# Cutting the opening transfers 1, 1, 1, 2, 3 in place of 1, 1, 1, 1, 2, 2 in an RMS-norm and matrix-product kernel

## Chip, cores, metric

The kernel runs on one core of one Trainium2 chip. The metric is the device time of one execution in microseconds (us). The span of a profile is shorter than this time by about 2 us.

## The reference

```python
# x: 16 x 1024 x 512, weight: 512 x 768, all float32
def reference(x, gamma, weight, eps):
    rms = np.sqrt(np.mean(x ** 2, axis=-1, keepdims=True) + eps)
    x_norm = x / rms * gamma
    return np.matmul(x_norm, weight).astype(np.float32)
```

The 16,384 rows are worked in 128 tiles of 128 rows. A tile of x has 256 KB, a tile of the output 384 KB.

## The kernel before

A tile is loaded by SyncE (SP), cast to bfloat16 on GpSimd (POOL), transposed on TensorE (PE) two bfloat16 at a time as one float32 word, and copied back from PSUM by VectorE (DVE). It is then multiplied by the scaled weights on TensorE. ScalarE (ACT) squares and sums the rows and takes the root; VectorE takes the reciprocal. The product is scaled by it on ScalarE (even tiles) or VectorE (odd tiles), and stored by SyncE. All loads and stores of x and the output go through the one queue of SyncE.

The lists below cut the tiles into transfers. The first 16 tiles are packed so that a transfer of n tiles gives each partition n neighbouring rows.

```python
    opening = [1, 1, 1, 1, 2, 2]
    last = NT // OG - 1                                   # NT = 128, XG = 16, OG = 8
    x_first, x_size = stretches(XG, {0: opening + [4, 4], 1: [4, 4, 8], 2: [8, 8]})   # others: 16
    o_first, o_size = stretches(OG, {0: opening, 1: [4, 4], last - 1: [4, 4],
                                     last: [2, 2, 1, 1, 1, 1]})                       # others: 8

    def rows(ap, i, n):
        if i < XG:
            return ap[i * P:(i + n) * P, :].rearrange("(p t) d -> p t d", t=n)
        return ap.rearrange("(g p t) d -> g p t d", p=P, t=XG)[i // XG, :, i % XG:i % XG + n, :]
    # ... cut ...
    def load(i):
        if i // XG not in x_tiles:
            x_tiles[i // XG] = xin.tile([P, XG, D], F32, name="xt")
        nc.sync.dma_start(out=held(x_tiles, XG, i, x_size[i]), in_=rows(x, i, x_size[i]))
    # ... cut ...
    def store(i):
        first, n = o_first[i], o_size[i]
        if i == first + n - 1:
            nc.sync.dma_start(out=rows(out, first, n), in_=held(o_tiles, OG, first, n))
```

The opening, and the head of the loop over pairs of tiles (pair j is tiles 2j and 2j+1):

```python
        load_weights(0)
        load_until(3)
        load_weights(1)
        load_until(2 * XG)
        # ... tiles 0 to 3, each alone; cut ...
        cast(6, nc.gpsimd, 2)
        cast(8, nc.gpsimd, 2)
        norms(4, 2)
        for j in range(2, NP):
            load_until(2 * j + AHEAD)                     # AHEAD = 20
            if j + 3 < NP:
                cast(2 * j + 6, nc.gpsimd, 2)
            if j < 4:
                norms(2 * j + 2, 2)                       # squares, root, reciprocal
            # ... cut ...
            for i, engine in ((2 * j, nc.scalar), (2 * j + 1, nc.vector)):
                a = accumulator()
                matmuls(i, a, range(K), feed)             # feed: transposes a later pair, then its copy
                finish_tile(i, a, engine)                 # scales, and stores when a stretch is full
```

Of the kernel before, what the change touches and what calls it, by code (L numbers as in the profile page):

```python
# [18 lines left out]
def kernel(  # L19
# [32 lines left out]
                i += n  # L52
        return first, size

    opening = [1, 1, 1, 1, 2, 2]
    last = NT // OG - 1
    x_first, x_size = stretches(XG, {0: opening + [4, 4], 1: [4, 4, 8], 2: [8, 8]})
    o_first, o_size = stretches(OG, {0: opening, 1: [4, 4], last - 1: [4, 4], last: [2, 2, 1, 1, 1, 1]})
# [290 lines left out]
```

## Time and profile before

| | before |
|---|---|
| time, median of 3 runs | 211.08 us (210.78 to 211.16) |
| span of the profiled run | 209.0 us |
| TensorE busy | 201.6 us, 96% of the span |
| queue of SyncE | 85.46 MB, 97.0% of 16 DMA engines' span |
| first matmul of tile 6 | 18.16 us, after 0.27 us of idle time |
| last issue of a store | 203.9 us |

A line of a group or a timeline gives start, length, engine, line of the kernel, operation, output <- input, and how many; the bracket is the idle time before it and what ended it. In the rows by slice a digit is the busy share in tenths. The lines that the argument began from stand in the prediction.

### The profile page before, as it was taken

What the parts mean: (1) busy time and instruction counts of PE and PEld (TensorE: products, weight loads), DVE (VectorE), ACT (ScalarE), POOL (GpSimd) and SP (SyncE); (2) the same over time, 40 slices, a digit from 0 to 9 for tenths busy, and PEclk for the clock granted to TensorE, in tenths of its full rate; (3) what the DMA queues carried; (4) which work ended last, traced back from release to release, by engine and by line L of the source; (5) the groups of instructions that cost most, each with busy time, mean ns of one, the idle gap of its engine ahead of it and who ended that gap; (6) DMA issues with size and microseconds to landing.
All of it is one profiled execution on the core that took longest, in us unless ns stands there. A gap on an engine that the chain in (4) does not pass through costs nothing.

```text
span 209.0 us, 3534 instructions
## 1 busy us (share of the span) xinstructions
PE 201.6 (96%) x1298; PEld 137.9 (66%) x1298; DVE 109.0 (52%) x173; ACT 149.6 (72%) x359; POOL 67.0 (32%) x73
## 2 busy tenths in 40 slices
PE   7999999999999999999999999999999999999980
PEld 2466777666766776667766776667667766677640
DVE  0465654654565465456545644654564465456550
ACT  2689987787778778777877777787777778777640
POOL 1357532306331073213623062310633045230000
PEclk9999999999999999999999999999999999999999
DMA  6999999999999999999999999999999999899994
GB/s 231 392 430 422 408 395 436 424 414 439 431 458 411 412 442 425 447 411 437 428 448 419 423 423 442 433 433 417 428 442 447 405 441 414 381 386 386 383 374 182
DMA packets 7077, 85.69 MB, mean 410 GB/s; under 512 B 786, under 2 KB 916, under 8 KB 3476
## 3 DMA queue, kind: packets, MB, share of 16 engines
q1 hardware_dynamic: 7056, 85.46, 97.0%
q8 instruction: 10, 0.16, 0.3%
q14 instruction: 7, 0.06, 0.1%
q10 hardware_dynamic: 4, 0.00, 0.0%
HBM read 35.13 MB, written 50.33 MB: 409 GB/s over the span
## 4 chain that ended last, share of the span: by engine, by line
PE 91%; ACT 3%; DMA 2%; POOL 1%; DVE 1%; issue 0%; SPq 0%
PE ops L168 77%; PE tp L133 13%; DMA xt<-in_x_dram 2%; ACT jk L98 1%; ACT ot L150 1%; POOL xb L94 1%; ACT rms L102 0%; DVE xT L140 0%; PE ops L227 0%; DVE ot L152 0%; SPq L206 0%; DVE rstd L104 0%
## 5 line engine op out<-in xcount | busy, mean ns | idle before, releaser
L168 PE MATMUL ops<-w_bf,xT 128*128 128x256 bf16 (+1 forms) x1024 | 194.2, 326 | 0.3 <-DVE xT L140 0.3
L168 PEld LDWEIGHTS <-xT 128*128 128x128 bf16 x1024 | 100.0, 98 | 56.4 <-DVE xT L140 1.4
L94 POOL CAST xb<-xt 128x1024 bf16<-128x1024 f32 (+1 forms) x67 | 66.3, 1002 | 118.9 <-PE tp L133 72.9
L150 ACT ACTIVATE ot<-ops,rstd 128x768 f32<-128x768 f32 (+1 forms) x65 | 58.1, 894 | 47.2 <-PE ops L168 47.2
L140 DVE COPY xT<-tp 128x1024 bf16<-128x1024 bf16 (+1 forms) x67 | 44.7, 667 | 83.3 <-PE tp L133 83.0
L98 ACT ACTIVATE jk<-xt 128x512 bf16<-128x512 f32 x128 | 78.7, 619 | 0.7 <-DMA xt<-in_x_dram 0.7
L133 PE MATMUL tp<-ident_f,xb 128*128 128x128 f32 x256 | 68.9, 273 | 0.1
L152 DVE TENSOR_SCALAR ot<-ops,rstd 128x768 f32<-128x768 f32 (+1 forms) x65 | 64.5, 993 | 2.9 <-PE ops L168 2.9
L133 PEld LDWEIGHTS tp<-ident_f,xb 128*128 128x128 f32 x256 | 35.9, 141 | 3.8 <-POOL xb L94 0.7
L98 ACT ACTIVATION_READ_ACCUMULATOR jk<-xt 128x1 f32 x128 | 24.4, 191 | 0.0
L102 ACT ACTIVATE rms<-ssq,eps_sb 128x4 f32<-128x4 f32 (+3 forms) x35 | 10.4, 297 | 1.1
L104 DVE RECIPROCAL rstd<-rms 128x4 f32<-128x4 f32 (+3 forms) x35 | 5.9, 167 | 3.3 <-ACT rms L102 3.3
L227 PE MATMUL ops<-warm 128*128 128x512 bf16 x16 | 6.4, 561 | 1.2 <-DVE eps_sb L220 1.2
L227 PEld LDWEIGHTS <-warm 128*128 128x128 bf16 x16 | 1.9, 131 | 3.9 <-issue 2.5
L150 ACT ACTIVATE w_bf<-w_f,g_sb 128x768 bf16<-128x768 f32 x2 | 1.9, 936 | 3.6 <-DMA w_f<-in_weight_dram 3.6
L201 ACT ACT_TABLE_LOAD x1 | 1.3, 1283 | 1.3 <-PEq L330 1.3
L152 DVE TENSOR_SCALAR w_bf<-w_f,g_sb 128x512 bf16<-128x512 f32 (+2 forms) x3 | 1.4, 485 | 1.1 <-DMA w_f<-in_weight_dram 1.0
L241 DVE COPY g_sb<-tp 128x4 f32<-128x4 f32 x1 | 0.2, 162 | 3.1 <-PE tp L239 3.1
L239 PEld LDWEIGHTS tp<-ident_f,g_row 2*128 2x128 f32 x2 | 0.3, 200 | 0.8 <-issue 0.8
L218 DVE MEMSET warm<- 128x256 uint32 x1 | 0.3, 272 | 0.9 <-PEq L330 0.9
L239 PE MATMUL tp<-ident_f,g_row 2*128 2x2 f32 x2 | 0.4, 264 | 0.0
masks.py:199 POOL TENSOR_SCALAR_AFFINE_SELECT ident_f<-ident_f 128x128 f32<-128x128 f32 x1 | 0.3, 292 | 0.1
(6 smaller groups left out, 0.7 us busy)
## 6 DMA issues: line engine op xcount, KB each, us to landing
out_dram<-ot SPq DMA_DIRECT2D x12, 3072.0 KB, 16.3
xt<-in_x_dram SPq DMA_DIRECT2D x5, 4096.0 KB, 23.0
xt<-in_x_dram SPq DMA_DIRECT2D x3, 2048.0 KB, 19.4
out_dram<-ot SPq DMA_DIRECT2D x4, 1536.0 KB, 11.6
xt<-in_x_dram SPq DMA_DIRECT2D x4, 1024.0 KB, 13.2
out_dram<-ot SPq DMA_DIRECT2D x4, 768.0 KB, 10.4
out_dram<-ot SPq DMA_DIRECT2D x7, 384.0 KB, 11.2
w_f<-in_weight_dram SPq DMA_DIRECT2D x2, 768.0 KB, 5.9
```

Of the source, the lines that this page charges most:

```text
L94: engine.tensor_copy(out=xb_tiles[i // 2][:, i % 2:i % 2 + n, :], in_=held(x_tiles, XG, i, n))
L98: nc.scalar.activation(out=jk, in_=held(x_tiles, XG, i)[:, 0, :], func=AF.Square, accum_out=ssq)
L102: nc.scalar.activation(out=rms[:, :n], in_=ssq[:, :n], func=AF.Sqrt, scale=1.0 / D, bias=eps_sb)
L104: nc.vector.reciprocal(out=rstd[:, :n], in_=rms[:, :n])
L133: nc.tensor.transpose(out=tp_tiles[j][:, t, h, :], in_=words[:, lo:lo + P], identity=ident_f)
L140: nc.vector.tensor_copy(out=dst[:, t:t + n, :], in_=src[:, t:t + n, :])
L150: nc.scalar.mul(out=dst, in_=src, mul=r)
L152: nc.vector.tensor_single_scalar(out=dst, in_=src, scalar=r, op=mybir.AluOpType.mult)
L168: nc.tensor.matmul(out=acc[:, lo:hi], lhsT=xT_tiles[i // 2][:, i % 2, k // 2, :, k % 2], rhs=w_bf[:, k, lo:hi], start=(k == 0), stop=(k == ...
L201: nc.scalar.preload_act_table(AF.Sqrt)
L227: nc.tensor.matmul(out=spare[:, :WIDE], lhsT=warm[:, :P], rhs=warm, start=True, stop=True)
L239: nc.tensor.transpose(out=gp[:, c, :], in_=g_row[:, :, c], identity=ident_f[:2, :2])
```

## The change

The intent is to save transfers, and so their fixed costs, in the opening: tiles 3 to 7 are moved in a pair and a triple.

```diff
-    opening = [1, 1, 1, 1, 2, 2]
+    opening = [1, 1, 1, 2, 3]
```

The one list cuts loads and stores alike. Three loads (tile 3; tiles 4, 5; tiles 6, 7) become two (3, 4; 5, 6, 7), and three stores become two.

## The prediction

> **What bounds the kernel now.** I read the page's table of busy time first, then the chain that ended last, then the timelines of single engines over the opening, because the change touches nothing after tile 7. From the page of the kernel before, the busy row of TensorE, the busy share of the DMA engines per slice, and the chain's shares by engine:
>
> ```profile
> PE 201.6 (96%) x1298; PEld 137.9 (66%) x1298; DVE 109.0 (52%) x173; ACT 149.6 (72%) x359; POOL 67.0 (32%) x73
> ...
> DMA  6999999999999999999999999999999999899994
> ...
> PE 91%; ACT 3%; DMA 2%; POOL 1%; DVE 1%; issue 0%; SPq 0%
> ```
>
> TensorE is busy 96% of the span and makes up 91% of the chain. From about 18 us it never idles: the only idle time the page shows in front of a matmul of line 168 is 0.3 us in all. A pair of tiles costs it 3.04 us (in the chain of waits the same group returns every 0.76 us, four to a pair). So whatever the opening gains or loses by the time TensorE enters this steady stretch goes one to one into the end. The DMA engines are nearly full as well, so a rival must be kept for them.
>
> What sets the entry into the steady stretch stands in the chain in order of time (start us, length us, what):
>
> ```profile
> 11.59 0.90 ACT ot L150
> 12.49 0.62 ACT jk L98 x2
> 13.11 0.02 issue
> 13.13 0.29 ACT rms L102
> 13.43 0.79 ACT ot L150
> 14.22 1.23 ACT jk L98 x4
> 15.45 0.02 issue
> 15.47 0.29 ACT rms L102
> 15.77 1.24 ACT jk L98 x4
> 17.00 0.02 issue
> 17.02 0.30 ACT rms L102
> ...
> 17.44 0.68 DVE xT L140
> 18.12 0.05 issue
> 18.16 0.39 PE ops L168
> ```
>
> From 11.59 to 17.32 us the path lies on ScalarE without a gap: scaling of tile 0, squares of tile 3, its root, scaling of tile 2, squares and root of tiles 4 and 5, then of 6 and 7. VectorE takes the reciprocal of that last root before it copies the transposed pair 6/7 (17.44), and TensorE, which has run dry, starts tile 6 at 18.16. No load is on this piece of the path. The line of that start in the timeline of TensorE says how long it had stood:
>
> ```profile
> 18.16 0.39 PE L168 MATMUL ops<-w_bf,xT 128*128 128x512 bf16 x1 [0.27 <-DVE xT L140]
> ```
>
> TensorE has 0.27 us of slack against ScalarE there. When the loads in question land is to be read from the casts on GpSimd, which wait for them (timeline of GpSimd; the bracket is the idle time before and who ended it):
>
> ```profile
> 10.76 0.61 POOL L94 CAST xb<-xt 128x512 bf16<-128x512 f32 x1 [1.90 <-DMA xt<-in_x_dram]
> 12.03 2.32 POOL L94 CAST xb<-xt 128x512 bf16<-128x512 f32 x3 [0.66 <-DMA xt<-in_x_dram]
> 15.90 2.02 POOL L94 CAST xb<-xt 128x1024 bf16<-128x1024 f32 x2 [1.55 <-DMA xt<-in_x_dram]
> ```
>
> The first is tile 3, the second tiles 4, 5 and the pair 6/7, the third follows the load of tiles 8 to 11. A cast begins 0.05 us after its load landed (the chain has 5.96 and 6.01 for the first), so tile 3 landed at 10.71, tiles 4/5 at 11.98, tiles 8 to 11 at 15.85. Tiles 6/7 left no wait; spread by bytes between the last two times they landed at 11.98 + 3.87/3 = 13.27.
>
> **What the Trainium skill says.** "DMA: Bandwidth & Descriptors", section "Rules for kernel authors", advises to coalesce small transfers and to make them at least 1 MiB. Its section "Anatomy of one DMA" (for another issuing path than this one) gives a fixed cost of about 2 us per transfer and says it is mostly the wait for the last byte's confirmation. That is latency, and here it is covered: the 512 KB of tiles 4/5 landed 1.27 us after tile 3, that is 413 GB/s, with no 2 us between two landings. So merging can save little where transfers stand in one full queue. Section "Why a DMA increments its semaphore by 16 and not by 1": only the full count says that all data landed. Hence a merged load gives its first tile up only with its last, which is the price of this change. "Perfetto Trace Analysis", section "Identifying the Most-Contended Engine", warns that matmul busy time misleads and wants the weight-load share, 66% here. I rely not on the 96% but on the absence of gaps after 18 us.
>
> **The change part by part.** The opening is cut 1,1,1,2,3 in place of 1,1,1,1,2,2, for loads and stores alike. The static order of instructions shows TensorE, VectorE, ScalarE and GpSimd unchanged; only the queue's changes: three loads (256, 512, 512 KB) become two (512, 768 KB), and three stores (384, 768, 768 KB) become two (768, 1152 KB). That is one transfer fewer each way, not two. The bytes stay the same.
>
> Loads. The queue is full (the stretch from 10 to 14 us moved 433 to 436 GB/s), so I keep the bytes' pace. Half of the old 1.27 us lies between tile 3 and tile 4: the pair 3/4 lands at 10.71 + 0.64 = 11.35, the triple where 6/7 landed, 13.27. Then, with casts of 0.62 us for one tile and 1.04 for two:
> - Cast 3: 11.40 to 12.01, before 10.76 to 11.37. Its weight load on TensorE stood at 11.93 and needs the cast's end plus 0.05 (8.85 to 8.90 for tile 2): 12.06, **0.13 later**. The matmuls of tile 3 waited for just this tile's copy, so TensorE carries the 0.13 on.
> - Cast 4 ends at 12.63, before 12.64: nothing.
> - Cast 5: 13.32 to 13.93; needed by TensorE at 13.82 before, now 13.98: 0.16 late in all.
> - Cast 6/7: 13.94 to 14.98; needed at 14.69 before, now 15.03: **0.34 late**. TensorE's work up to tile 5 ends 0.34 later.
> - The slack takes 0.27 of this: 0.34 - 0.27 = **0.07 us** remain.
> ScalarE: squares of tile 3 start at 12.39 and the load lands at 11.35; tile 5 at 14.73 against 13.27; tile 6 at 15.68 against 13.27. The scaling of tile 2 needs matmuls that ended near 12.91, now 13.04, and ScalarE is not free before 13.42. So ScalarE's path doesn't move. VectorE copies pair 6/7 at 17.44 and its last transpose would end at 16.80 + 0.34 = 17.14: still waiting for the reciprocal.
>
> Stores. Tile 3's was issued at 15.94, and now goes with tile 4's near 18.15 (its scaling on ScalarE ends at 18.11). Tile 5's was issued at 19.10 and now goes with 6/7's at 22.5, as that did before. All these wait in the queue behind loads of tiles up to 31, which run until some 28 us by bytes (the 2 MB of tiles 24 to 31 alone take about 5 us at 410 GB/s after tiles 20 to 23). So nothing is moved later. Saved issues: one of about 0.35 us (median of the load issues) on SyncE, which isn't on the path.
>
> Sum: 211.08 + 0.07 = 211.15, called **211.2 us**.
>
> **The rivals.**
> 1. Fewer, larger transfers speed up the queue. If each saved 0.1 to 0.2 us, the triple would land that much earlier and TensorE's lateness would shrink below the slack of 0.27: no loss, and no gain either, as ScalarE's path needs no load here. Time: 211.0 to 211.1.
> 2. The merged pair lands as late as tiles 4/5 did, at 11.98, because its two halves interleave with what follows. Then cast 3 ends at 12.64, TensorE is late by 12.69 - 11.93 = 0.76, ScalarE's scaling of tile 2 by about 0.25, and after the slack 0.76 - 0.27 = 0.49 remains: 211.6. Against it: the earlier loads landed one after the other at the pace of their bytes.
> 3. DMA becomes the bound. Each transfer's semaphore is shared with the eighth one before it, so one transfer fewer shifts all later pairings. Tiles 24 to 31 now wait for tile 2's load (cast at 8.24) in place of the second weights (10.02); the queue is full then, so this gains nothing. Later, GpSimd waits 43.9 us in all for loads, and the load of tile 48 is cast at 72.87 for transposes near 75.9 by the 3.04 us pace: 2 us of slack after the cast. A load pushed back by more than that would stall TensorE, perhaps 1 us each. But those loads are issued on release of a buffer by squares on ScalarE (10.1 us of such waits in the queue's own view), which follow TensorE. Small chance: 212 to 213.
> 4. The tail: the DMA share between 185 and 200 us is 0.87 to 0.95, so no backlog from the opening reaches the end; nothing.
>
> **Range and chances.** Point 211.2; rivals 1 and 2 span 211.0 to 211.6; the three runs before differ by 0.38 us. 8 in 10: 210.6 to 211.8. Two per cent are 4.2 us, more than any rival gives: faster 0.01, same 0.98, slower 0.01.
>
> **What would show it.** In the changed kernel's trace: cast of tile 3 near 11.40, of tile 5 near 13.32, of 6/7 near 13.94; ScalarE gapless from 11.6 to 17.3 as before; copy of pair 6/7 at 17.44; first matmul of tile 6 between 18.16 and 18.3 with its idle time gone or nearly so; 3.04 us a pair after that, without gaps. It is wrong if tile 3's cast starts after 11.9, if ScalarE shows a wait for a load between 12 and 17 us, or if TensorE stalls near 51, 76 or 100 us.

## The result, and the profile after

The changed kernel took 210.51 us (median of 6 runs, 210.23 to 211.06), the kernel before in the same rounds 210.95 us (6 runs with the first three, 210.43 to 211.16). The ratio is 0.9986, with a 95% interval from 0.9967 to 1.0006: the same. A ratio here is the mean time of one kernel's fast runs over that of the other's in the same rounds, so it isn't quite the ratio of the medians.

The page of the changed kernel, rows that answer to those of before (TensorE's busy time, the DMA share by slice, the chain by engine); 25 matmul records are missing from this trace, as the count 1273 shows:

```profile
PE 199.3 (96%) x1273; PEld 137.4 (66%) x1298; DVE 109.0 (52%) x173; ACT 149.5 (72%) x359; POOL 67.0 (32%) x73
...
DMA  6999999999999999999999999999999999899895
...
PE 90%; ACT 3%; DMA 2%; issue 1%; POOL 1%; DVE 1%; SPq 0%
```

The chain in order of time over the opening (start, length, what):

```profile
11.45 0.90 ACT ot L150
12.35 0.62 ACT jk L98 x2
...
15.63 1.24 ACT jk L98 x4
16.86 0.02 issue
16.89 0.30 ACT rms L102
...
17.30 0.68 DVE xT L140
17.98 0.05 issue
18.02 0.39 PE ops L168
```

It is the chain of before, piece by piece, 0.14 us earlier throughout. That shift was there before any changed transfer mattered: ScalarE scaled tile 0 at 11.45 in place of 11.59, behind weights that had landed 0.14 us earlier. The casts on GpSimd, and TensorE's start on tile 6:

```profile
11.20 1.17 POOL L94 CAST xb<-xt 128x512 bf16<-128x512 f32 x2 [2.51 <-DMA xt<-in_x_dram]
13.08 1.60 POOL L94 CAST xb<-xt 128x512 bf16<-128x512 f32 x2 [0.71 <-DMA xt<-in_x_dram]
15.67 2.02 POOL L94 CAST xb<-xt 128x1024 bf16<-128x1024 f32 x2 [0.99 <-DMA xt<-in_x_dram]
```

```profile
18.02 0.39 PE L168 MATMUL ops<-w_bf,xT 128*128 128x512 bf16 x1 [0.24 <-DVE xT L140]
```

The first cast line is now tiles 3 and 4, the second tile 5 and the pair 6/7. Tile 3 is cast 0.44 us later than before, tiles 6 and 7 0.33 us later (13.64 in place of 13.31). TensorE's idle time ahead of tile 6 shrank by only 0.03 us, from 0.27 to 0.24. So the opening cost nothing that can be seen; 0.07 us had been predicted.

But between the two profiled runs the span fell by 0.5 us, 208.98 to 208.45, while the last store was issued only 0.14 us earlier. Most of the difference lies behind TensorE's last work. The stretches of the tail show it. The columns are the stretch, its length, busy time of PE, PEld, DVE, ACT and POOL with the number of instructions, the granted clock, **the DMA share as a mean of 16 engines**, and GB/s. First before, then after:

```profile
205.00:206.00 1.00, 0.00 (x0) 0.00 (x0) 0.00 (x0) 0.00 (x0) 0.00 (x0) 1.00 0.97 366
206.00:207.00 1.00, 0.00 (x0) 0.00 (x0) 0.00 (x0) 0.00 (x0) 0.00 (x0) 1.00 0.21 79
207.00:208.00 1.00, 0.00 (x0) 0.00 (x0) 0.00 (x0) 0.00 (x0) 0.00 (x0) 0.98 0.06 23
```

```profile
205.00:206.00 1.00, 0.00 (x0) 0.00 (x0) 0.00 (x0) 0.00 (x0) 0.00 (x0) 0.77 0.88 330
206.00:207.00 1.00, 0.00 (x0) 0.00 (x0) 0.00 (x0) 0.00 (x0) 0.00 (x0) 0.50 0.18 68
207.00:208.00 1.00, 0.00 (x0) 0.00 (x0) 0.00 (x0) 0.00 (x0) 0.00 (x0) 0.50 0.02 6
```

A share of 0.06 is one engine of 16, and 0.21 is about three. In the kernel before, most DMA engines are done at about 206 us, and a few, in the end one, go on to 207.6 us. The packet records of the trace say the same: at 206.5 us three packets are in flight, at 207.0 two, at 207.5 one, and those at 206.5 and 207.0 are, but for one, still of sizes 3072 and 2048 bytes, that is, of earlier stores, while the rest has written the last store (1024 bytes). These late engines became the question of the experiments.

### The profile page after: what moved, and what is told of

The parts are those of the page before. It is cut to its first block, busy times and chain, and to the rows that moved or that the text cites. A ratio compares the mean times of both kernels' runs of the same rounds, so it can differ in the third digit from the quotient of the medians.

```text
span 208.4 us, 3506 instructions
## 1 busy us (share of the span) xinstructions
PE 199.3 (96%) x1273; PEld 137.4 (66%) x1298; DVE 109.0 (52%) x173; ACT 149.5 (72%) x359; POOL 67.0 (32%) x73
## 4 chain that ended last, share of the span: by engine, by line
PE 90%; ACT 3%; DMA 2%; issue 1%; POOL 1%; DVE 1%; SPq 0%
PE ops L168 77%; PE tp L133 13%; DMA xt<-in_x_dram 2%; ACT jk L98 1%; ACT ot L150 1%; POOL xb L94 1%; ACT rms L102 0%; DVE xT L140 0%; PE ops L227 0%; DVE ot L152 0%; SPq L206 0%; DVE rstd L104 0%
## 5 line engine op out<-in xcount | busy, mean ns | idle before, releaser
L168 PE MATMUL ops<-w_bf,xT 128*128 128x512 bf16 (+1 forms) x999 | 192.7, 324 | 1.5 <-DVE xT L140 0.2
L227 PE MATMUL ops<-warm 128*128 128x512 bf16 x16 | 5.2, 474 | 1.2 <-DVE eps_sb L220 1.2
```

The costliest lines, as they stand in the source:

```text
L168: nc.tensor.matmul(out=acc[:, lo:hi], lhsT=xT_tiles[i // 2][:, i % 2, k // 2, :, k % 2], rhs=w_bf[:, k, lo:hi], start=(k == 0), stop=(k == ...
L227: nc.tensor.matmul(out=spare[:, :WIDE], lhsT=warm[:, :P], rhs=warm, start=True, stop=True)
```

## The experiments

Theory P is the prediction's: TensorE's entry into its steady stretch goes one to one into the end. Its rival became theory Q: the queue, in the end its slowest engines, sets the end, and transfers cost it time. The table has, for each profiled run, the last issue of a store, the time by which 104 of the 128 packets of the last store were written (13 engines' share, at 8 packets each), the end of the last packet, and the span. The packet records don't name the engine; that the last three groups of 8 packets belong to three engines is inferred from the packets in flight. (In thirteen the last store is cut otherwise, and its 104th packet isn't the end of 13 engines' share.)

| run | transfers against before | last store issued | 104 packets written | last packet | span | median us (before beside it) | ratio, 95% interval |
|---|---|---|---|---|---|---|---|
| before | | 203.88 | 206.12 | 207.65 | 209.0 | | |
| the change | -2 | 203.74 | 205.98 | 207.18 | 208.4 | 210.51 (210.95) | 0.9986, 0.9967 to 1.0006 |
| after_again | -2 | 204.24 | 206.49 | 207.60 | 208.8 | 210.56 (210.91) | 0.9984, 0.9968 to 1.0001 |
| loads_only | -1 | 203.87 | 206.11 | 207.57 | 209.0 | 210.77 (210.91) | 0.9992, 0.9980 to 1.0004 |
| stores_only | -1 | 203.68 | 205.93 | 207.50 | 208.9 | 210.66 (210.91) | 0.9986, 0.9972 to 0.9999 |
| load_five | -2 | 205.47 | 207.61 | 208.27 | 209.4 | 211.18 (210.91) | 1.0017, 1.0002 to 1.0032 |
| split_mid | +10 | 206.18 | 208.35 | 208.97 | 210.4 | 212.12 (210.79) | 1.0054, 1.0037 to 1.0071 |
| fine_tail | +2 | 204.02 | 206.29 | 207.56 | 209.1 | 210.74 (210.79) | 0.9992, 0.9976 to 1.0008 |
| five_tail | 0 | 205.62 | 207.76 | 208.09 | 209.4 | 210.97 (210.79) | 0.9999, 0.9983 to 1.0016 |
| root_late_after | -2 | 203.36 | 205.59 | 207.27 | 208.5 | 210.35 (210.79) | 0.9979, 0.9959 to 0.9998 |
| load_quarters | +15 | 204.24 | 206.48 | 208.56 | 209.9 | 211.87 (210.81) | 1.0045, 1.0031 to 1.0058 |
| merged | -4 | 204.52 | 207.01 | 207.36 | 208.8 | 210.48 (210.81) | 0.9983, 0.9970 to 0.9995 |
| thirteen | +1 | 205.68 | 207.47 | 208.03 | 209.7 | 211.45 (210.81) | 1.0030, 1.0017 to 1.0042 |
| merged_root | -4 | 203.31 | 205.83 | 207.69 | 209.1 | 210.64 (210.81) | 0.9984, 0.9970 to 0.9998 |

### The change again, and its halves

after_again is the changed kernel. loads_only and stores_only take one half of the change each:

```diff
-    opening = [1, 1, 1, 1, 2, 2]
+    opening = [1, 1, 1, 2, 3]              # loads_only; stores_only: as before
+    o_opening = [1, 1, 1, 1, 2, 2]         # loads_only; stores_only: [1, 1, 1, 2, 3]
-    o_first, o_size = stretches(OG, {0: opening, 1: [4, 4], ...
+    o_first, o_size = stretches(OG, {0: o_opening, 1: [4, 4], ...
```

> The changed kernel again, on the chip of the three runs that follow. My theory: it costs what the kernel before costs, and the 0.44 us between the medians of the first comparison is mostly scatter (run to run 0.7 us): ratio 0.998 to 1.002. Rival (the merged transfers themselves save time, through the load or the store queue): ratio 0.998 or below with an interval that leaves out 1.

> The loads cut 1,1,1,2,3 and the stores as before. My theory: first matmul of tile 6 at the same distance from the landing of tile 0 as before (12.2 us) within 0.1 us, TensorE still 0.2 us idle ahead of it; time within 0.15 us of before. Rival (fewer loads help): that distance shrinks by 0.1 us or more.

> The stores cut 1,1,1,2,3 and the loads as before. My theory: these stores wait behind queued loads and nobody waits for them, so time within 0.15 us of before and loads of tiles 32 and later landing within 0.5 us of before. Rival (fewer stores free the queue earlier): the load of tile 32, cast at 47.39 us before, is cast 0.5 us or more earlier, as it was in the changed kernel (46.60), and the time falls by 0.3 us.

The three were 0.9984, 0.9992 and 0.9986 of before; only the interval of stores_only leaves 1 out, barely. The results of loads_only, stores_only and the next run were wrong. In the first 16 tiles the packing of rows depends on the cut, so a load and a store that are cut differently put rows in the wrong place. Number, size and order of all work are as meant.

TensorE's start on tile 6 was 18.16 us in loads_only (before: 18.16) and 17.97 in stores_only, with 0.27 and 0.28 us of idle time ahead of it. The distance from the landing of tile 0 was 12.21 us in loads_only against 12.20 before: merged loads gave TensorE nothing and took nothing. The rival of stores_only named two signs, an earlier load of tile 32 and a time 0.3 us shorter, and both came (cast at 46.25; 0.25 us between the medians). But loads_only had the same early load (46.39), and so had a later run with the loads and stores of before in the opening (46.42, split_mid). So that sign is scatter and can't count for it. What stays is a time a little short in every run with fewer transfers, too small to be told from noise one by one.

### Five tiles in one load

```diff
-    opening = [1, 1, 1, 1, 2, 2]
+    opening = [1, 1, 1, 5]                 # loads; stores as before
```

> Tiles 3 to 7 loaded in one transfer, stores as before: the price of a merged load made large. My theory: all five land where the triple did, near 13.05; tile 3 is cast 13.1 to 13.7, TensorE transposes it 1.8 us later than before, less the slack of 0.25 us ahead of tile 6: first matmul of tile 6 1.5 us later, time about 1.5 us longer (ratio 1.007). ScalarE shows a wait of about 0.8 us for tile 3's load and later one for TensorE ahead of tile 2's scaling. Rival (the opening is hidden behind the full DMA queue, which sets the end): time the same within 0.3 us though tile 6 starts later.

The first half came as worked out. All five tiles were cast from 13.11 us on, TensorE transposed tile 3 1.7 us later, and started tile 6 1.6 us later (its chain in order of time):

```profile
3.31 9.75 DMA xt<-in_x_dram
13.06 0.05 issue
13.11 0.62 POOL xb L95
13.74 0.04 issue
13.78 0.44 PE tp L134 x2
...
19.03 0.68 DVE xT L141
19.71 0.05 issue
19.76 0.39 PE ops L169
```

The last store was issued 1.6 us later too (205.47). But the span grew by 0.4 us and the time by 0.17% (0.36 us, 0.04 to 0.67). Theory P had asked for 1.5 us, the rival for 0.3 at most. The tail says where the rest went:

```profile
206.00:207.00 1.00, 0.00 (x0) 0.00 (x0) 0.00 (x0) 0.00 (x0) 0.00 (x0) 1.00 0.99 386
207.00:208.00 1.00, 0.00 (x0) 0.00 (x0) 0.00 (x0) 0.00 (x0) 0.00 (x0) 1.00 0.62 232
208.00:209.00 1.00, 0.00 (x0) 0.00 (x0) 0.00 (x0) 0.00 (x0) 0.00 (x0) 0.56 0.02 6
```

Here the engines finish almost together: 104 packets by 207.61, the last at 208.27. Before it was 206.12 and 207.65. The bulk of the queue follows TensorE, 2.2 us behind the last issue in both. The last engine doesn't: TensorE's delay was largely spent on time in which it was still catching up. This refutes theory P, and it is where theory Q was formed.

The packet records of the kernel before show this more directly. Three times near the end most engines run dry and wait for TensorE's next store, while a few go on: from 181.3 to 181.8, from 193.0 to 193.9 and from 199.7 to 200.0 us between three and five packets are in flight, and never none. The stretch in the middle, in the columns of above:

```profile
193.10:193.90 0.80, 0.80 (x7) 0.56 (x6) 0.07 (x1) 0.48 (x1) 0.00 (x0) 1.00 0.25 108
```

A share of 0.25 is four engines of 16. Packets of one engine follow each other closely, so the last engine can be traced back from its end at 207.65: down to 176.8 us each of its packets starts 3 or 4 ns before the end of the one before, straight through all three dry stretches. The one exception is a packet of 16 KB of the instruction queue (q8 on the page) at 194.66 us, which kept this engine for 0.95 us. In load_five the last engine's packets likewise lead back to such a packet, at 195.17 us. So these packets are a part of what keeps an engine late; the rest isn't shown.

### More transfers in the middle, more near the end, and an earlier TensorE

split_mid is the kernel before with the stores of tiles 16 to 95 in halves; fine_tail and five_tail cut the last stores finer; root_late_after takes ScalarE off TensorE's path ahead of tile 6.

```diff
 # split_mid (on before)
-    ... {0: opening, 1: [4, 4], last - 1: [4, 4], ...
+    ... {0: opening, **{g: [4, 4] for g in range(1, 12)}, last - 1: [4, 4], ...
 # fine_tail (on the change); five_tail has opening = [1, 1, 1, 5] as well
-    ... last - 1: [4, 4], last: [2, 2, 1, 1, 1, 1]})
+    ... last - 3: [4, 4], last - 2: [4, 4], last - 1: [2, 2, 2, 2], last: [2, 2, 1, 1, 1, 1]})
 # root_late_after (on the change)
-            if j < 4:
+            late = None
+            if j == 2:
+                late = stats.tile([P, 4], F32, name="ssq")
+                for t in range(2):
+                    square(2 * j + 2 + t, late[:, t:t + 1])
+            elif j < 4:
                 norms(2 * j + 2, 2)
 ...
                 matmuls(i, a, range(K), feed)
+                if late is not None and i % 2:
+                    root(2 * j + 2, 2, late)
                 finish_tile(i, a, engine)
```

> The kernel before, with the stores of tiles 16 to 95 cut in halves: ten transfers more, in the middle of the run, results right. Theory Q, formed after the first runs (the DMA queue, more closely the slowest of its 16 rings, is never empty and sets the end; each transfer costs each ring 8 packets and one semaphore write at a fixed 9 ns, 0.08 us): time longer by 10 x 0.08 = 0.8 us, ratio 1.004, first and last matmul where they were. Theory P, that of my prediction (TensorE's entry into its steady stretch goes one to one into the end): time the same within 0.2 us.

split_mid took 0.54% longer, more than Q's 0.4%, but not for Q's reason alone, and the expectation that TensorE would stay where it was missed. SyncE issues in program order, and the loads of 16 tiles now stood behind a half store that waits for VectorE. The load of tile 48 was issued at 53.96 us in place of 49.84 and cast at 76.95 in place of 72.87. TensorE ran out of casts (the waits of this run):

```profile
POOL xb L94 <- DMA xt<-in_x_dram: 76.0, 14, 11.8
...
PE tp L133 <- POOL xb L94: 1.6, 2, 1.3
```

The last store came 2.3 us later. The run is confounded as a test of Q. It does show the danger that the prediction had named as its third rival: with this load 4 us later, TensorE waited 1.6 us for casts.

> The changed kernel, with the stores of tiles 96 to 111 cut in fours and of 112 to 119 in twos: four transfers more, near the end, results right. Theory Q: the slowest ring was busy anyway, so four transfers more cost 4 x 0.08 = 0.3 us or nothing, no gain. Variant D (the whole queue runs dry between 180 and 195 us for want of stores, where the DMA share is 0.83 to 0.98): finer stores fill it, and the end comes 0.9 us earlier than in the changed kernel.

fine_tail was no faster than the change (0.9992 of before, the change 0.9986 and 0.9984). The queue as a whole was fuller between 180 and 190 us (a share of 1.01 and 1.00, against 0.88 and 0.98 in the change), but emptier between 195 and 200 us (0.70 against 0.93): the finer stores moved the idle time rather than removed it. The last packet still came at 207.56. Variant D's 0.9 us did not come. This run alone doesn't say why; the dry stretches above do: the idle time in the mean share is not on the engine that ends last.

> Tiles 3 to 7 loaded and stored in one transfer, with the finer stores of the run before near the end; results right. TensorE enters its steady stretch 1.6 us later, as in the earlier run with one load of five. Theory P: 1.5 us or more over the run before. Theory Q: 0.3 us over it or less, as the last issue of a store comes 1.6 us later but the slowest ring still has work then.

TensorE's last store came 1.6 us later than in fine_tail, and the time grew by 0.07% (0.15 us) by the two ratios, though with two transfers fewer, which load_quarters below puts at some 0.1 us. Theory P asked for 1.5 us. It falls a second time, here with right results.

> The changed kernel, with the root and the reciprocal for tiles 6 and 7 moved behind the copy of that pair, so that TensorE does not wait for ScalarE ahead of tile 6; results right. Both theories: first matmul of tile 6 about 0.25 us earlier (17.8 where it was 18.02), its idle time gone, and with no slack left the merged loads' lateness, some 0.03 to 0.1 us, stays in it. Theory P: time 0.25 us shorter than the changed kernel's. Theory Q: the same as the changed kernel's within 0.1 us, the time between the last issue of a store and the end longer by 0.25 us.

The mechanism was as expected: TensorE went from tile 5 to tile 6 without a gap (first matmul at 17.65 us, 0.37 earlier than in the change), and the last store was issued 0.38 us earlier than in the change. The last packet came at 207.27, in the change at 207.18; the spans are 208.5 and 208.4. The ratio, 0.9979, is 0.0005 to 0.0007 below that of the change, 0.1 to 0.15 us, on another chip and inside the intervals. In the profiles the earlier TensorE was spent on a longer tail, which is what Q says; a small gain isn't excluded by the times.

### The cost of a transfer by itself

In the packet records of the kernel before, packets of 2048, 4096, 6144 and 8192 bytes take 84, 159, 234 and 312 ns (medians), over the first three 75 ns for each 2048 bytes and **9 ns a packet**. The 4-byte packets that announce an engine's share of a transfer take 9 ns too. A transfer of 128 partitions has 8 packets and one announcement on each of 16 engines, so theory Q took its fixed part, whatever its size, as 9 x 9 = 81 ns of each engine's time. That is too much, because an engine's packets overlap by 3 to 4 ns. From start to start, the last engine's 2048-byte packets stand 80 ns apart and its 1024-byte packets 42.4, which leaves 5 ns a packet; an announcement takes 6 ns. By that estimate a transfer costs 8 x 5 + 6 = 46 ns. load_quarters tests the size, in a place where nothing else moves: each load of 16 tiles is cut in four, issued back to back.

```diff
-        nc.sync.dma_start(out=held(x_tiles, XG, i, x_size[i]), in_=rows(x, i, x_size[i]))
+        n = 4 if x_size[i] == XG else x_size[i]
+        for t in range(i, i + x_size[i], n):
+            nc.sync.dma_start(out=held(x_tiles, XG, t, n), in_=rows(x, t, n))
```

> The kernel before, with each of the five loads of sixteen tiles cut in four loads of four tiles, issued back to back in the same place; results right. Fifteen transfers more, 120 data packets and 15 semaphore writes more on each of the 16 rings. The tail of the earlier traces says what to look at: 13 of the rings write their share of the last store together, some 2.2 us after its issue, and three come late, the last one up to 1.7 us later. Theory Q (that last ring never idles and sets the end): its end moves by 15 x 0.08 = 1.2 us, from 207.6 to 208.8; time longer by about 1 us, ratio 1.005, TensorE and the last issue of a store where they were (203.9). Rival (transfers cost nothing where the queue holds work): time the same within 0.2 us.

The time grew by 0.45% (0.31 to 0.58), that is 0.95 us (0.65 to 1.22), or 0.063 us for each of the 15 transfers. Both 15 x 0.046 = 0.7 us and 15 x 0.08 = 1.2 us lie in this interval, the rival's 0.2 us doesn't. TensorE wasn't hurt: it had 0.28 us of idle time ahead of tile 6 as before, the last store was issued 0.36 us later (the opening of this run came that much late by chance), and 104 packets were written 0.36 us later. The three late engines moved more: their last packets ended at 207.25, 208.06 and 208.55 in place of 206.78, 207.34 and 207.64. The tail:

```profile
206.00:207.00 1.00, 0.00 (x0) 0.00 (x0) 0.00 (x0) 0.00 (x0) 0.00 (x0) 0.71 0.50 183
207.00:208.00 1.00, 0.00 (x0) 0.00 (x0) 0.00 (x0) 0.00 (x0) 0.00 (x0) 0.50 0.14 53
208.00:209.00 1.00, 0.00 (x0) 0.00 (x0) 0.00 (x0) 0.00 (x0) 0.00 (x0) 0.50 0.04 13
```

Two engines at work between 207 and 208 us (0.14), less than one after (0.04), all others idle. So a transfer's fixed part reaches the end of this kernel, though the queue holds work all the time and TensorE never waits for it. This is the run that tells the two theories apart in a quantity well clear of noise.

### Fewer still, and a look for something faster

```diff
 # merged (on the change)
-    x ... 1: [4, 4, 8], 2: [8, 8]})
+    x ... 1: [8, 8], 2: [8, 8]})
-    o ... last: [2, 2, 1, 1, 1, 1]})
+    o ... last: [2, 2, 2, 1, 1]})
 # thirteen (on the change), store of tile 126 and the two parts of tile 127
+    for a, b in ((0, 104), (104, P)):      # partitions a to b of each
 # merged_root: merged, with the edit of root_late_after
```

> The changed kernel with two transfers fewer still: tiles 16 to 23 loaded in one transfer in place of two, tiles 124 and 125 stored in one in place of two; results right. Theory Q: 4 x 0.08 = 0.3 us less than before in all, ratio 0.9985, half of it owed to the change under study; the last issue of a store where it was. Rival (only scatter): ratio 1.000 with the changed kernel's 0.9985 a chance.

merged was 0.9983 of before, with an interval that leaves 1 out; Q had 0.9985. With four transfers fewer it is as fast as the change with two, within noise. In the profiled run the opening was late by chance (first matmul of tile 6 at 18.69, last store issued at 204.52 where 203.7 was expected), and the last packet still came at 207.36.

> The changed kernel with the last three stores (tiles 126 and 127) each cut in partitions 0 to 103 and 104 to 127; results right. The Trainium skill says that such cuts run on the first 13 and the first 12 rings. A look for a faster version: if the three late rings are the last three, they are spared, and the end comes with the 13 others, 0.4 to 0.7 us earlier than in the changed kernel though three transfers are added. If a late ring is among the first 12, it has a quarter more of these stores to write and the end comes 0.3 to 0.5 us later.

thirteen was slower, 1.0030. By the Trainium skill, "DMA: Bandwidth & Descriptors", section "Why a DMA increments its semaphore by 16 and not by 1", a copy of 104 partitions runs on 13 engines, the lowest-numbered. The 779 announcements in this trace (16 for each of 44 transfers, 25 for each of three pairs) agree with 13 and 12 engines. No run here shows which engines they were. What spoiled the test is plainer: SyncE had six issues to make in place of three, the last came at 205.68 in place of 203.74, and all engines were held by that. Which engines, by number, are late stays open.

> The version that the runs point to: the changed kernel with the two further merges and with the root and the reciprocal of tiles 6 and 7 behind the copy of that pair; results right. Theory Q: 0.3 us less than before, as with the merges alone (ratio 0.998 to 0.9985); the earlier TensorE adds nothing. Theory P would add another 0.25 to 0.3 us (ratio 0.997).

merged_root was 0.9984, as merged alone. TensorE's last store came at 203.31, the earliest of all runs, and the last packet at 207.69, as late as in the kernel before. Some 0.0015 to 0.002 below 1 is what all the right-resulted versions with two or four transfers fewer in all reach (the change, merged, merged_root, root_late_after). None is clearly faster than the change.

## Why the prediction was right or wrong, point by point

**The time.** The forecast "the same" was right. 211.2 us had been predicted from a kernel before at 211.08. In the joint rounds both kernels' medians were lower, and 210.51 is just below the stated low end of 210.6; the ratio applied to 211.08 gives 210.8, inside. The predicted difference was +0.07 us; the two comparisons of the change give -0.30 (-0.70 to +0.13) and -0.34 us (-0.67 to +0.02), so the sign probably missed.

**"Whatever the opening gains or loses ... goes one to one into the end."** This step failed. A TensorE that was 1.6 us late cost 0.4 us of span (load_five) and 0.15 us of time (five_tail against fine_tail). The error has a place in the prediction: in rival 4 a DMA share of 0.87 to 0.95 was read as a queue without backlog. It is the mean of 16 engines, and a few of them were behind all the time. The Trainium skill, "Perfetto Trace Analysis", section "Identifying the Most-Contended Engine", which the prediction cited for TensorE, says of DMA that 16 engines make occupancy misleading; this trace agrees (0.06 in the last stretch was the whole path). That TensorE had no gaps after 18 us was true, and did not mean that TensorE set the end. The chain of waits also put 90% on TensorE and didn't show this: it follows the last store's issue back to TensorE, and has no way to go through packets of other stores on one late engine.

**The loads.** They landed as worked out: the pair at 11.15 in place of 11.35, the triple at 13.03 in place of 13.27, of which 0.14 is the shift of the whole opening. ScalarE's path had no gap, VectorE still waited for the reciprocal, and TensorE shows no wait near 51, 76 or 100 us. Rival 2 (pair at 11.98) fell.

**TensorE's lateness ahead of tile 6.** 0.34 us was mis-sized; 0.03 us was measured (transposes of tile 6 at 14.79, against 14.90 less the shift of 0.14). I had followed weight loads. In the kernel before, the weight load for tile 6 stood at 14.69 and its matmul at 14.90: weight loads run ahead, and only what exceeds this lead of 0.21 us delays TensorE. In the changed kernel it stood at 14.73, 0.06 ahead of its matmul. So all of the lateness was hidden before the slack of 0.27 was touched; the remainder of 0.07 us was too much, and the idle time ahead of tile 6, which was to be gone or nearly so, was still 0.24 us.

**The saved transfers.** The prediction booked them as nothing but one issue (there are two, a load and a store). Each is worth about 0.06 us at the end (load_quarters), about 0.05 by the packet records, so two are worth 0.09 to 0.13 us. That is rival 1, though not in the way it stated: the gain doesn't come through an earlier load, but through the work of the last engine. Whether it explains all of the measured 0.3 us can't be said; the intervals are wider than the question.

**Rival 3.** Not met by the change, but real: split_mid delayed loads by 4 us and TensorE stalled.

**What stays open.** That the last engine works without a break is read from its packets for the last 31 us of the kernel before. For the time before, and for the other runs, it is inferred from two facts, that the end follows the number of transfers and hardly follows TensorE. The records don't name engines, so which ones are late isn't shown, and why they are late only in part.

## What to carry to other kernels

Where a queue moves bytes for nearly the whole span, look at how the DMA share falls off in the last microseconds: a long tail at 1/16 or 3/16 suggests that a few late engines set the end, and that a faster compute engine will gain little. There, each transfer that can be merged without delaying a need saves its fixed part, here about 0.05 to 0.06 us; merging is worth it in tens, not in twos. The gain has an end, too: the other engines finished 1.5 us before the last one here (206.12 and 207.65), and they do follow TensorE. Before merging loads, find the first consumer and its slack: here the price was hidden by weight loads that ran 0.2 us ahead and by a TensorE that waited for ScalarE anyway.

## What the Trainium skill lacked or had wrong

- "DMA: Bandwidth & Descriptors", "Anatomy of one DMA": the fixed cost of a transfer is given as about 2 us of latency, for the path issued from GpSimd. In a full queue of SyncE a transfer's fixed part was 0.063 us (15 transfers added 0.95 us), and about 0.046 us by the packet records. Beside figures for single packets the page has none for a transfer in a full queue.
- The same page, "Specifications": a limit of about 358 GB/s for HBM per core. This core moved 409 GB/s over the span, with reads and writes mixed, and 430 to 436 in the stretch from 10 to 14 us. The page's own later note, that this limit is for two busy cores, agrees better.
- The same page, "Latency and other measured facts", says that engines 7 and 15 are usually slower, and ties it to transfers issued from GpSimd. Here all large transfers were issued from SyncE, and about three of 16 engines were late by 0.7 to 1.5 us at the end in the kernel before. The records don't say whether engines 7 and 15 were among them.
- "Perfetto Trace Analysis", "What "DMA-bound" means": specific DMA engines are listed among what can bind, which fits here, but no page has the sign by which late engines are found in the mean share: 1/16 in the last stretch (0.06 from 207 to 208 us).
